# Sums of rows for seven-product blocks moved to VectorE and begun half a block ahead, norms one tile later, more lane steps per k-step

## The chip, the cores and the metric

The kernel runs on one core of one Trainium2 chip. The metric is the device time of one execution in microseconds (us). The engines are called as the profile calls them: PE is TensorE (PEld its weight load), DVE is VectorE, ACT is ScalarE, POOL is GpSimd, SP is the queue that issues most transfers. Every engine takes its instructions in the order in which they stand in its queue: an instruction that waits holds all that stand behind it.

## The reference, cut to what matters

One layer of an encoder, for two groups of tokens (256 and 1024, so 10 tiles of 128 tokens) with shared weights:

```
hn   = rms_norm(x, norm_g)
proj = hn @ w_in            # xbc, z_ssd, dt, q, k, v, z_att, mq, z_mem
y    = ssd_scan(forward) + ssd_scan(backward) + d_skip * xs
yg   = (y * silu(z_ssd)) in 2 groups of 512
o_ssd = rms_norm(yg, ssd_norm_g)
o_att = window_attention(q, k, v, sink) * silu(z_att)
o_mem = attention of mq to the normed memory * silu(z_mem)
out  = x + concat[o_ssd, o_att, o_mem] @ w_out      # 2048 x 2048
```

All of it is in float32.

## The kernel before, in words

Large products are blocks. `block_tok` makes 5 tiles of 128 tokens by up to 512 columns in 5 PSUM banks (`acc`), over 16 k-steps of 128 rows of the weight; `block_feat` does the same with features and tokens exchanged. Each float32 product is made of three products of rounded halves: ACT rounds the weight (`wh`), DVE takes the rest (`wl`), in `wsplit` (lines 215 and 216), and PE does high x high, low x high, high x low (lines 263 to 265 of `block_tok`). So a k-step of `block_tok` has 15 matmuls. The last two k-steps are done together, bank by bank, so that the evacuations are spread out. `wh` and `wl` have 3 buffers each, the raw weights 4.

The smaller work (attention, the scan, norms) runs beside the blocks. It is written as Python generators in two lanes. After each k-step, `pump` lets each lane do as many steps as `RATES` gives, a pair of numbers for each kind of block; fractions are carried on. The order in which instructions stand on each engine comes from the order in which they are written, from `high_priority` (which puts the splits and the evacuations ahead), and from the scheduler of the framework.

`ssd_up` goes up the tiles of the scan, `ssd_down` comes down them. `ssd_down(t)` loads `yd`, `zd` and the state, adds the backward part (`pyb` on PE, then `y` and `yd` on DVE), multiplies by the gate, takes the sum of squares on ACT (`yss`), makes the factor `yrs` on POOL, and scales `yd` to `yn` on DVE. `turn_ssd` transposes `yn` on PE (`pr`), copies it on ACT (`so`) and stores it in DRAM (`oT`). Tiles 9 and 8 come last of all in the lanes.

The output product `w_out` has two halves. The first 5 tiles of tokens were refilled into `xH`/`xL` (by `refill_o`, beside the block before) and run as four blocks `tok("o")`, called c=0 to c=3 here. The other 5 tiles run as 8 `block_pair`s, which make a 2 x 2 product of blocks with seven products in place of eight. These need sums of blocks on both sides: for the weights, four sums `ws` of 128x128 for each of 8 k (line 1126, on POOL), split as `sh`/`sl`; and for the rows, four sums `tt` of 128x320 for each of 8 k. One of these 8 is called a seven here. `seven_load` loads `ra` and `rb` of a seven from `oT`, `seven_sums` scales `rb` on ACT (line 1038) and makes the four sums (line 1043), `seven_rows` and `seven_split` split everything into `rH` (ACT, line 1047) and `rL` (DVE, line 1048). `ra`, `rb` and two of the five output tiles of a block (`yt`) share the 3 buffers with the tag `ch`. The rows of sevens 4 to 7 lie where the quads of `xH`/`xL` were, so that they can be written only when the last block is through with a quad.

`plan` says at which k-step of block c=3 each part is written: before, seven k has its sums and first splits at k-step 2k + 1, its loads at 2k - 1. All lanes are emptied and their memory is freed (`beside.close()`) ahead of that block.

Of the kernel before, what the change touches and what calls it, by code (L numbers as in the profile page):

```python
# [10 lines left out]
F32 = mybir.dt.float32  # L11
# [5 lines left out]
ALU = mybir.AluOpType  # L17
AX = mybir.AxisListType

P = 128  # L20
# [8 lines left out]
CH, WB, RB, WA, WBB = 3, 3, 4, 5, 4  # L29
RBB = 3  # L30

RATES = ({'q': (1.9, 0), 'kv': (1.3, 0), 'za': (1.2, 0.5), 'x': (1.1, 0.5), 'mq': (1.1, 1.2), 'zm': (1.1, 1.2),
          'z0': (1.2, 1.2), 'z1': (1.2, 1.2)},
         {'kv': (1.0, 1.0), 'x': (0.9, 1.05), 'q': (1.3, 2.3), 'za': (1.3, 2.3), 'z0': (1.5, 2.5), 'z1': (1.5, 2.5),
          'mq': (1.5, 2.6), 'zm': (1.5, 2.6), 'o': (1.7, 1.65)})
NEG = -1e30

C_X, C_Z, C_DT, C_Q, C_K, C_V, C_ZA, C_MQ, C_ZM = 0, 1536, 2560, 2592, 3104, 3232, 3360, 3872, 4384
# [4 lines left out]
def hymba_encoder_kernel(  # L43
# [24 lines left out]
    beside = ExitStack()  # L68
# [77 lines left out]
    lanes = (deque(), deque())  # L146
# [10 lines left out]
    def step(lane):  # L157
        name, gen = lane[0]
        try:

            with ExitStack() as st:
                for ins in marks:
                    st.enter_context(tc.issue_after(ins))
                next(gen)
        except StopIteration:
            lane.popleft()
            done.add(name)
# [68 lines left out]
    def w_out_rows(c):  # L236
        return w_laid(w_out_laid[c], 512)

    def block_tok(w, nt, evac, before_last=None):

        load, n = w
        ps = [acc.tile([P, 512], F32, tag="acc", name="acc") for _ in range(nt)]
        hls = {}
        for k in range(KT):
            raw = wp.tile([P, 512], F32, tag="wraw", name="wraw", bufs=RB)
            load(k, raw[:, :n])
            with tc.high_priority(offset=HP[2]):
                h = wp.tile([P, 512], F32R, tag="wh", name="wh", bufs=WB)
                l = wp.tile([P, 512], F32R, tag="wl", name="wl", bufs=WB)
                wsplit(raw[:, :n], h[:, :n], l[:, :n])  # L250
            hls[k] = h, l
            if k == KT - 2:
                continue
            if k == KT - 1 and before_last is not None:
                before_last(k)

            for t in range(nt):
                for k_ in ((k - 1, k) if k == KT - 1 else (k,)):
                    q, m = divmod(k_, 4)
                    h, l = hls[k_]  # L260
                    sh = cur["H", q][:, m, t * P:(t + 1) * P]
                    sl = cur["L", q][:, m, t * P:(t + 1) * P]
                    T.matmul(ps[t][:, :n], sh, h[:, :n], start=(k_ == 0), stop=False)  # L263
                    T.matmul(ps[t][:, :n], sh, l[:, :n], start=False, stop=False)  # L264
                    T.matmul(ps[t][:, :n], sl, h[:, :n], start=False, stop=(k_ == KT - 1))  # L265
                if k == KT - 1:
                    with tc.high_priority(offset=HP[0]):
                        evac(t, ps[t])
            if k == KT - 1:
                yield k - 1  # L270
            yield k
# [113 lines left out]
    def ev_out(c0):  # L385
        def f(t, ps):

            if t in (0, 3):
                yt = rp.tile([P, 640], F32, tag="ch", name="yt", bufs=CH)[:, :512]
            else:  # L390
                yt = ev.tile([P, 512], F32, tag="evt" if t == 2 else "evu", name="yt")
            S.dma_start(yt, xrow(t)[:, c0:c0 + 512])
            V.tensor_add(yt, ps, yt)
            S.dma_start(y_first[t * P:(t + 1) * P, c0:c0 + 512], yt)
        return f
# [550 lines left out]
        yield  # L946


    normed = deque()

    def turn_ssd():

        if normed:
            t, g, n = normed.popleft()
            ps = psum("pr")
            for j in range(4):
                T.transpose(ps[:, j * P:(j + 1) * P], n[:, j * P:(j + 1) * P], ident)
            o = mp.tile([P, 512], F32, tag="rb", name="so", bufs=RBB)
            A.activation(o, ps, AF.Copy)
            S.dma_start(oT_d[2 + g][t // 5][:, :, t % 5 * P:(t % 5 + 1) * P], hv(o, 4))  # L960

    def ssd_down(t):
        first = t in (0, NS)
        last = t in (NS - 1, NT - 1)
        tok = slice(t * P, (t + 1) * P)
        ss = sm.tile([P, 2], F32, tag="s2", name="yss", bufs=4)
        if not last:
            cc = mp.tile([P, 2, P], F32, tag="btok", name="cc", bufs=1)
            S.dma_start(cc, xbc_d[10:12, :, tok].rearrange("f p c -> p f c"))
        ld = []  # L970
        for g in range(2):
            c = slice(g * 512, (g + 1) * 512)
            y = mp.tile([P, 512], F32, tag="ya", name="yd", bufs=2)
            S.dma_start(y, yp_d[t][:, c])
            z = mp.tile([P, 512], F32, tag="xs", name="zd", bufs=2)
            S.dma_start(z, z_d[g][t])
            st = None
            if not first:
                st = state[:, c] if last else wb("st2")
                S.dma_start(st, sb_d[t][:, c])  # L980
            ld.append((y, z, st))
        turn_ssd()
        yield
        turn_ssd()
        yield
        yield
        for g in range(2):
            c = slice(g * 512, (g + 1) * 512)
            y, z, st = ld[g]
            if not last:  # L990
                pf = psum("pyb")
                T.matmul(pf, cc[:, g, :], state[:, c], start=True, stop=True)
                y2 = wb("y3")
                V.tensor_mul(hv(y2), hv(pf), hb(eacs_all[:, t, 16 + 8 * g:24 + 8 * g], 8, 64))
                V.tensor_add(y, y, y2)
            V.tensor_mul(y, y, z)
            A.activation(z, y, AF.Square, scale=rxh[:, t:t + 1], accum_out=ss[:, g:g + 1])
            if not first and not last:
                V.tensor_mul(hv(state[:, c]), hv(state[:, c]), hb(cd_all[:, t, 16 + 8 * g:24 + 8 * g], 8, 64))
                V.tensor_add(state[:, c], state[:, c], st)  # L1000
            yield
        rs = sm.tile([P, 2], F32, tag="s2", name="yrs", bufs=4)
        rsqrt(rs, ss, 1.0 / 512, 2)
        G.tensor_scalar(out=rs, in0=rs, scalar1=rxh[:, t:t + 1], scalar2=None, op0=ALU.mult)
        yield
        yield
        for g in range(2):
            n = mp.tile([P, 512], F32, tag="rf", name="yn", bufs=2)
            V.tensor_scalar(out=n, in0=ld[g][0], scalar1=rs[:, g:g + 1], scalar2=None, op0=ALU.mult)
            normed.append((t, g, n))  # L1010
        yield
        if first:
            yield
            turn_ssd()
            yield
            turn_ssd()
            yield

# [15 lines left out]
    def seven_sums(k):  # L1036
        a, b = raw[k]
        A.activation(b, b, AF.Copy, scale=vec[:, R_SG + k:R_SG + k + 1])
        a, b = hv(a, 2), hv(b, 2)
        t, u = sums[k] = [fin.tile([P, 2, 320], F32, tag="tt", name="tt", bufs=4) for _ in range(2)]  # L1040
        for o, x, y in ((t[:, 0], a[:, 1], a[:, 0]), (u[:, 0], b[:, 1], a[:, 1]), (t[:, 1], b[:, 1], t[:, 0]),
                        (u[:, 1], b[:, 0], t[:, 1])):
            G.tensor_tensor(out=o, in0=x, in1=y, op=ALU.subtract)

    def in_two(k, c, src):
        h, l = [x[:, c] for x in rows[k]]
# [14 lines left out]
        in_two(k, slice(1 + 2 * i, 3 + 2 * i), sums[k][i])  # L1061


    plan = {}
    for k in range(8):
        for j, f, args in ((-1, seven_load, ()), (1, seven_sums, ()), (1, seven_rows, ()), (2, seven_split, (0,)),
                           (3, seven_split, (1,))):

            late = k == 7 and f in (seven_rows, seven_split)
            plan.setdefault(2 * k + j + late, []).append((f, k) + args)  # L1070

    def beside_step(j):
        with ExitStack() as st:
            for ins in marks:
                st.enter_context(tc.issue_after(ins))
            for f, *args in sorted(plan.get(j, ()), key=lambda x: (x[0] is seven_load, x[1])):
                f(*args)
# [268 lines left out]
    queue(0, mem_attn, range(5, 8))  # L1346
    queue(0, mem_swap, [0])
    queue(0, mem_attn, range(8, 10))
    for c in range(3):
        tok("o", w_out_rows(c), ev_out(c * 512), grp=1)  # L1350
    for x in lanes:
        while x:
            step(x)
    beside.close()
    fin = ctx.enter_context(tc.tile_pool(name="fin", bufs=2))
    beside_step(-1)
    for k in block_tok(w_out_rows(3), 5, ev_out(1536), before_last=lambda _: beside_step(14)):
        if k != 14:
            beside_step(k)
    for u in range(8):  # L1360
        for k in block_pair(u):
            if u == 0 and k < 3:
# [70 lines left out]
```

## Time and profile before

| what | value |
|---|---|
| median of 3 runs | 1866.29 us (1865.01 to 1867.31) |
| profiled execution | 1865.38 us |
| its span, first to last instruction | 1863.7 us |
| PE busy | 1838.3 us, 99% |
| DVE / ACT / POOL busy | 1158.4 / 824.3 / 260.2 us |
| mean clock granted to PE | 0.995 |

PE is busy nearly all the time, so time is to be found where PE is idle or runs below its full clock. The rows of PE give an idle time before an instruction and who ended it. Busy shares of the other engines count only where PE waits for them. The end of a matmul is modelled, and matmuls overlap, so their pace is read from the distance of their starts.

### The profile page before, as it was taken

What the parts mean: (1) busy time and instruction counts of PE and PEld (TensorE: products, weight loads), DVE (VectorE), ACT (ScalarE), POOL (GpSimd) and SP (SyncE); (2) the same over time, 40 slices, a digit from 0 to 9 for tenths busy, and PEclk for the clock granted to TensorE, in tenths of its full rate; (3) what the DMA queues carried; (4) which work ended last, traced back from release to release, by engine and by line L of the source; (5) the groups of instructions that cost most, each with busy time, mean ns of one, the idle gap of its engine ahead of it and who ended that gap; (6) DMA issues with size and microseconds to landing.
All of it is one profiled execution on the core that took longest, in us unless ns stands there. A gap on an engine that the chain in (4) does not pass through costs nothing.

```text
span 1863.7 us, 29965 instructions
## 1 busy us (share of the span) xinstructions
PE 1838.3 (99%) x10786; PEld 1649.2 (88%) x10786; DVE 1158.4 (62%) x2284; ACT 824.3 (44%) x1865; POOL 260.2 (14%) x435
## 2 busy tenths in 40 slices
PE   9999999999999999999999999999999999989999
PEld 7889999998998889999979987777888888779999
DVE  5434555766456666586776675676875554676665
ACT  6653333434534555334345545544464442443332
POOL 0010000000000000000000000000100000577775
PEclk9999999999999999999999999999999999989999
DMA  8774444443432564434435446467685573654442
GB/s 289 236 229 128 123 148 136 136 121 95 147 125 84 171 186 142 138 101 122 129 115 169 143 128 181 122 197 216 196 253 155 169 211 115 192 161 142 142 134 88
DMA packets 198452, 289.49 MB, mean 155 GB/s; under 512 B 18912, under 2 KB 80416, under 8 KB 198304
## 3 DMA queue, kind: packets, MB, share of 16 engines
q1 hardware_dynamic: 198160, 287.53, 50.8%
q8 instruction: 85, 1.39, 0.3%
q14 instruction: 63, 0.52, 0.1%
q10 hardware_dynamic: 144, 0.06, 0.0%
HBM read 230.59 MB, written 56.92 MB: 154 GB/s over the span
## 4 chain that ended last, share of the span: by engine, by line
PE 91%; DVE 3%; DMA 2%; ACT 2%; POOL 2%; issue 1%; SPq 0%; ACTq 0%; DVEq 0%; POOLq 0%
PE acc L263 13%; PE acc L265 13%; PE acc L264 13%; PE acc L298 10%; PE acc L300 10%; PE acc L299 10%; PE acc L1143 2%; PE acc L1144 2%; PE acc L1145 2%; PE py L901 2%; PE po L648 1%; PE ppt L638 1%; PE accm L1145 1%; PE accm L1144 1%; PE pmo L749 1%
## 5 line engine op out<-in xcount | busy, mean ns | idle before, releaser
L216 DVE TENSOR_TENSOR wl<-wraw,wh 128x512 fp32r<-128x512 f32 (+2 forms) x480 | 329.6, 687 | 369.1 <-ACT wh L215 358.0
L215 ACT ACTIVATE wh<-wraw 128x512 fp32r<-128x512 f32 (+2 forms) x480 | 287.2, 600 | 503.9 <-PE acc L265 220.8
L263 PE MATMUL acc<-wh,xH 128*128 128x512 f32 (+1 forms) x1248 | 487.0, 391 | 5.7 <-ACT wh L215 4.8
L264 PE MATMUL acc<-wl,xH 128*128 128x512 f32 (+1 forms) x1248 | 474.9, 381 | 5.6 <-DVE wl L216 5.5
L265 PE MATMUL acc<-wh,xL 128*128 128x512 f32 (+1 forms) x1248 | 475.1, 381 | 0.0
L298 PE MATMUL acc<-xH,wh 128*128 128x320 f32 x1280 | 401.4, 314 | 0.0
L299 PE MATMUL acc<-xL,wh 128*128 128x320 f32 x1280 | 395.9, 309 | 0.0
L300 PE MATMUL acc<-xH,wl 128*128 128x320 f32 x1280 | 395.8, 309 | 0.0
L263 PEld LDWEIGHTS acc<-wh,xH 128*128 128x128 f32 x1248 | 235.6, 189 | 54.4 <-ACT wh L215 7.1
L264 PEld LDWEIGHTS acc<-wl,xH 128*128 128x128 f32 x1248 | 235.7, 189 | 51.5 <-DVE wl L216 9.0
L265 PEld LDWEIGHTS acc<-wh,xL 128*128 128x128 f32 x1248 | 235.4, 189 | 43.6 <-issue 0.5
L298 PEld LDWEIGHTS acc<-xH,wh 128*128 128x128 f32 x1280 | 240.4, 188 | 3.6 <-issue 3.3
L299 PEld LDWEIGHTS acc<-xL,wh 128*128 128x128 f32 x1280 | 240.4, 188 | 1.6 <-issue 1.2
L300 PEld LDWEIGHTS acc<-xH,wl 128*128 128x128 f32 x1280 | 240.2, 188 | 0.3 <-issue 0.2
L215 ACT ACTIVATE sh<-ws 128x512 fp32r<-128x512 f32 x64 | 39.7, 631 | 126.7 <-POOL ws L1126 80.6
L216 DVE TENSOR_TENSOR sl<-ws,sh 128x512 fp32r<-128x512 f32 x64 | 50.7, 792 | 67.4 <-ACT sh L215 66.5
L372 DVE SCALAR_TENSOR_TENSOR c<-u,vec,c 128x638 f32<-128x638 f32 (+1 forms) x96 | 84.7, 882 | 0.7
L1126 POOL TENSOR_TENSOR ws<-wraw 128x128 f32<-128x128 f32 x128 | 72.4, 585 | 51.6 <-DVE sl L216 32.2
L210 DVE SCALAR_TENSOR_TENSOR xL<-chd,vec,xH 128x640 fp32r<-128x640 f32 (+1 forms) x56 | 46.8, 845 | 38.2 <-ACT xH L209 37.7
L884 ACT ACTIVATE rb<-rb,wj_all 128x128 f32<-128x128 f32 x160 | 52.5, 391 | 30.0 <-DMA rb<-ac 30.0
L136 POOL TENSOR_SCALAR qr<-qss 128x8 f32<-128x8 f32 x10 | 3.5, 352 | 437.5 <-DVE qss L572 437.4
L621 ACT ACTIVATE lg<-lg,nm 128x384 f32<-128x384 f32 (+1 forms) x80 | 45.0, 563 | 40.8 <-DVE nm L615 40.8
(330 smaller groups left out, 2702.5 us busy)
## 6 DMA issues: line engine op xcount, KB each, us to landing
wraw<-in_w_in_laid_dram SPq DMA_DIRECT2D x288, 256.0 KB, 2.8
wraw<-in_w_out_laid_dram SPq DMA_DIRECT2D x64, 256.0 KB, 3.2
wraw<-in_w_out_pairs_dram SPq DMA_DIRECT2D x64, 256.0 KB, 2.8
chd<-in_x_turned_dram SPq DMA_DIRECT2D x32, 320.0 KB, 4.7
rf<-ac SPq DMA_DIRECT2D x40, 256.0 KB, 3.7
rb<-ac SPq DMA_DIRECT2D x40, 256.0 KB, 4.1
wraw<-in_w_mem_laid_dram SPq DMA_DIRECT2D x32, 256.0 KB, 4.3
xst<-in_x_sample_dram SPq DMA_DIRECT2D x32, 256.0 KB, 4.4
```

Source lines behind the costliest of these rows:

```text
L215: a = A.activation(h, raw, AF.Copy)
L216: b = V.tensor_sub(l, raw, h.bitcast(F32))
L263: T.matmul(ps[t][:, :n], sh, h[:, :n], start=(k_ == 0), stop=False)
L264: T.matmul(ps[t][:, :n], sh, l[:, :n], start=False, stop=False)
L265: T.matmul(ps[t][:, :n], sl, h[:, :n], start=False, stop=(k_ == KT - 1))
L298: T.matmul(o, sh, cur["H", q][:, m, c], start=(k == 0), stop=False)
L299: T.matmul(o, sh, cur["L", q][:, m, c], start=False, stop=False)
L300: T.matmul(o, sl, cur["H", q][:, m, c], start=False, stop=(k == KT - 1))
L372: V.scalar_tensor_tensor(out=c[:, :n], in0=u[:, k:k + n], scalar=cw[k], in1=c[:, :n], op0=ALU.mult, op1=ALU.add)
L1126: G.tensor_tensor(out=o, in0=x, in1=y, op=op)
L1144: T.matmul(ps[p], h, xl, start=False, stop=False)
L1145: T.matmul(ps[p], l, xh, start=False, stop=(k_ == 7))
```

## The change

Four things are changed together. The four sums of a seven go from POOL to DVE. The sevens begin in the middle of block c=2: sevens 0 to 3 have their sums at k-steps 2k - 5 of block c=3 (a negative number is in c=2), sevens 4 to 6 at 4k - 11, seven 7 at 15; the lanes are emptied ahead of k=8 of c=2. The norm of a tile in `ssd_down` (`norm_ssd`) is written at the start of the next tile in place of the end of its own, and its transposes two and three steps after that. And all rates from the convolution blocks on are some 4% higher.

```diff
-RATES = ({'q': (1.9, 0), 'kv': (1.3, 0), 'za': (1.2, 0.5), 'x': (1.1, 0.5), 'mq': (1.1, 1.2), 'zm': (1.1, 1.2),
+RATES = ({'q': (1.9, 0), 'kv': (1.3, 0), 'za': (1.2, 0.5), 'x': (1.15, 0.5), 'mq': (1.15, 1.25), 'zm': (1.15, 1.25),
...
-          'mq': (1.5, 2.6), 'zm': (1.5, 2.6), 'o': (1.7, 1.65)})
+          'z1': (1.55, 2.6), 'mq': (1.55, 2.7), 'zm': (1.55, 2.7), 'o': (1.75, 1.8)})
...
+    def norm_ssd():
+        if "y" in tail:
+            t, ys, rs = tail.pop("y")
+            for g in range(2):
+                n = mp.tile([P, 512], F32, tag="rf", name="yn", bufs=2)
+                V.tensor_scalar(out=n, in0=ys[g], scalar1=rs[:, g:g + 1], scalar2=None, op0=ALU.mult)
+                tail[g] = t, n
...
     def ssd_down(t):
...
+        norm_ssd()
+        yield
...
-        turn_ssd()
-        yield
-        turn_ssd()
-        yield
+        yield
+        turn_ssd(0)
+        yield
+        turn_ssd(1)
         yield
...
-        for g in range(2):
-            n = mp.tile([P, 512], F32, tag="rf", name="yn", bufs=2)
-            V.tensor_scalar(out=n, in0=ld[g][0], scalar1=rs[:, g:g + 1], scalar2=None, op0=ALU.mult)
-            normed.append((t, g, n))
+        tail["y"] = t, [x[0] for x in ld], rs
...
-            G.tensor_tensor(out=o, in0=x, in1=y, op=ALU.subtract)
+            V.tensor_sub(o, x, y)
...
-        for j, f, args in ((-1, seven_load, ()), (1, seven_sums, ()), (1, seven_rows, ()), (2, seven_split, (0,)),
-                           (3, seven_split, (1,))):
+        at = 2 * k - 5 if k < 4 else 4 * k - 11 if k < 7 else 15
+        end = at + (k == 7)
+        for j, f, args in ((at - (2 if k < 4 else 4), seven_load, ()), (at, seven_sums, ()), (end, seven_rows, ()),
+                           (end + 1, seven_split, (0,)), (end + 2, seven_split, (1,))):
...
-    for c in range(3):
+    for c in range(2):
         tok("o", w_out_rows(c), ev_out(c * 512), grp=1)
...
+    for c in range(2, 4):
+        j0 = 16 * (c - 3)
+        for k in block_tok(w_out_rows(c), 5, ev_out(c * 512), before_last=lambda _: beside_step(j0 + 14)):
+            if j0 + k == -8:
+                for x in lanes:
+                    while x:
+                        step(x)
+                beside.close()
+                fin = ctx.enter_context(tc.tile_pool(name="fin", bufs=2))
+            if j0 + k < -8:
+                pump(RATES[1]["o"])
+            elif k != 14:
+                beside_step(j0 + k)
```

The order of POOL at the end of block c=3 and the start of the pairs, before:

```order
L1043 TENSOR_TENSOR tt<-rb__17104,tt 128x320
L1126 TENSOR_TENSOR ws<-wraw 128x128 x2
L1126 TENSOR_TENSOR ws<-ws,wraw 128x128
L1126 TENSOR_TENSOR ws<-wraw,ws 128x128
L1043 TENSOR_TENSOR tt<-rb__17167,ra 128x320
L1043 TENSOR_TENSOR tt<-rb__17167,tt 128x320
L1043 TENSOR_TENSOR tt<-ra 128x320
L1043 TENSOR_TENSOR tt<-rb__17167,tt 128x320
L1126 TENSOR_TENSOR ws<-wraw 128x128 x2
```

And now, from the last `yrs` of the scan on:

```order
L1015 TENSOR_SCALAR yrs<-yrs,rxh 128x2
L1135 TENSOR_TENSOR ws<-wraw 128x128 x2
L1135 TENSOR_TENSOR ws<-ws,wraw 128x128
L1135 TENSOR_TENSOR ws<-wraw,ws 128x128
L1135 TENSOR_TENSOR ws<-wraw 128x128 x2
```

Between the sums of the weights of two k-steps stood the four sums of a seven (17167 is seven 6); now nothing stands there.

The order of DVE behind the last tile of `ssd_down` (tile 8), before, where block c=2 ends (`yt` are its evacuations) and c=3 begins:

```order
L996 TENSOR_TENSOR yd<-yd,zd 128x512
L1009 TENSOR_SCALAR yn<-yd,yrs 128x512 x2
L216 TENSOR_TENSOR wl<-wraw,wh 128x512 x2
L393 TENSOR_TENSOR yt<-acc,yt 128x512 x4
L216 TENSOR_TENSOR wl<-wraw,wh 128x512
L393 TENSOR_TENSOR yt<-acc,yt 128x512
L216 TENSOR_TENSOR wl<-wraw,wh 128x512 x2
L1048 TENSOR_TENSOR rL<-ra,rH 128x320
L216 TENSOR_TENSOR wl<-wraw,wh 128x512
L1048 TENSOR_TENSOR rL<-rb__16788,rH 128x640
```

And now, in the middle of c=2 (the `wl` are those of k=11 and 12, of 13 and of 14; 16642 is seven 0, the second `tt<-ra` belongs to seven 1):

```order
L957 TENSOR_SCALAR yn<-yd,yrs 128x512 x2
L216 TENSOR_TENSOR wl<-wraw,wh 128x512 x2
L1051 TENSOR_TENSOR tt<-ra 128x320
L1056 TENSOR_TENSOR rL<-ra,rH 128x320
L216 TENSOR_TENSOR wl<-wraw,wh 128x512
L1051 TENSOR_TENSOR tt<-rb__16642,ra 128x320
L1051 TENSOR_TENSOR tt<-rb__16642,tt 128x320
L1051 TENSOR_TENSOR tt<-ra 128x320
L1051 TENSOR_TENSOR tt<-rb__16642,tt 128x320
L1056 TENSOR_TENSOR rL<-rb__16642,rH 128x640
L1056 TENSOR_TENSOR rL<-tt,rH 128x640
L216 TENSOR_TENSOR wl<-wraw,wh 128x512
```

The sums and splits of the sevens have moved ahead of the end of c=2, and the splits of the weights for its last k-steps now stand behind sums that need `rb`. The evacuations of c=2 come further down, in the same way between sums and splits of sevens 2 and 3.

On PE, the last `pyb` of tile 8 and its transposes `pr` had 60 matmuls of c=2 between them; now there are 19, since the last steps of the lane are written at once.

More of the change, by code (lines that the diff above doesn't have):

```diff
@@ L30 @@
 RBB = 3
-RATES = ({'q': (1.9, 0), 'kv': (1.3, 0), 'za': (1.2, 0.5), 'x': (1.1, 0.5), 'mq': (1.1, 1.2), 'zm': (1.1, 1.2),
-          'z0': (1.2, 1.2), 'z1': (1.2, 1.2)},
-         {'kv': (1.0, 1.0), 'x': (0.9, 1.05), 'q': (1.3, 2.3), 'za': (1.3, 2.3), 'z0': (1.5, 2.5), 'z1': (1.5, 2.5),
-          'mq': (1.5, 2.6), 'zm': (1.5, 2.6), 'o': (1.7, 1.65)})
+RATES = ({'q': (1.9, 0), 'kv': (1.3, 0), 'za': (1.2, 0.5), 'x': (1.15, 0.5), 'mq': (1.15, 1.25), 'zm': (1.15, 1.25),
+          'z0': (1.25, 1.25), 'z1': (1.25, 1.25)},
+         {'kv': (1.05, 1.05), 'x': (0.95, 1.1), 'q': (1.35, 2.4), 'za': (1.35, 2.4), 'z0': (1.55, 2.5),
+          'z1': (1.55, 2.6), 'mq': (1.55, 2.7), 'zm': (1.55, 2.7), 'o': (1.75, 1.8)})
 NEG = -1e30
@@ L946, in ssd_up, with turn_ssd @@
         yield
[L949 to L954, printed above, removed]
+    tail = {}
+    def norm_ssd():
[5 more added lines that the diff above has]
+                tail[g] = t, n
+    def turn_ssd(g):
+        if g in tail:
+            t, n = tail.pop(g)
             ps = psum("pr")
@@ L1004, in ssd_down @@
         G.tensor_scalar(out=rs, in0=rs, scalar1=rxh[:, t:t + 1], scalar2=None, op0=ALU.mult)
+        tail["y"] = t, [x[0] for x in ld], rs
         yield
         yield
-        for g in range(2):
-            n = mp.tile([P, 512], F32, tag="rf", name="yn", bufs=2)
-            V.tensor_scalar(out=n, in0=ld[g][0], scalar1=rs[:, g:g + 1], scalar2=None, op0=ALU.mult)
-            normed.append((t, g, n))
-        yield
         if first:
+            norm_ssd()
             yield
-            turn_ssd()
             yield
-            turn_ssd()
-            yield
+            for g in range(2):
+                turn_ssd(g)
+                yield
     seven = {1: (0, 0, 0), 2: (0, 1, 5), 6: (1, 1, 2), 5: (1, 0, 1), 3: (1, 3, 6), 7: (1, 2, 3), 4: (0, 2, 4)}
@@ L1065, in hymba_encoder_kernel @@
     for k in range(8):
-        for j, f, args in ((-1, seven_load, ()), (1, seven_sums, ()), (1, seven_rows, ()), (2, seven_split, (0,)),
-                           (3, seven_split, (1,))):
-            late = k == 7 and f in (seven_rows, seven_split)
-            plan.setdefault(2 * k + j + late, []).append((f, k) + args)
+        at = 2 * k - 5 if k < 4 else 4 * k - 11 if k < 7 else 15
+        end = at + (k == 7)
+        for j, f, args in ((at - (2 if k < 4 else 4), seven_load, ()), (at, seven_sums, ()), (end, seven_rows, ()),
+                           (end + 1, seven_split, (0,)), (end + 2, seven_split, (1,))):
+            plan.setdefault(j, []).append((f, k) + args)
     def beside_step(j):
@@ L1348, in hymba_encoder_kernel @@
     queue(0, mem_attn, range(8, 10))
-    for c in range(3):
+    for c in range(2):
         tok("o", w_out_rows(c), ev_out(c * 512), grp=1)
[L1351 to L1359, printed above, removed]
+    for c in range(2, 4):
[11 more added lines that the diff above has]
+                beside_step(j0 + k)
     for u in range(8):
```

## The prediction

> **What bounds the kernel now.** I read the page's first two parts, then what TensorE waits for, then stretches, then single rows.
>
> ```profile
> PE 1838.3 (99%) x10786; PEld 1649.2 (88%) x10786; DVE 1158.4 (62%) x2284; ACT 824.3 (44%) x1865; POOL 260.2 (14%) x435
> ...
> POOL 0010000000000000000000000000100000577775
> PEclk9999999999999999999999999999999999989999
> ```
>
> TensorE (PE) is busy 99%, so only its idle time and its slow clock can be won: some 25 us of idle, and one slice of forty below full clock. That slice is where POOL first works hard, the last block of `tok("o")`, c=3. In windows of 10 us (columns: length, then busy of PE, PEld, DVE, ACT and POOL with counts, clock, DMA share, GB/s):
>
> ```profile
> 1590.00:1600.00 10.00, 10.00 (x49) 8.35 (x47) 3.92 (x6) 2.94 (x6) 0.87 (x1) 1.00 0.90 282
> ...
> 1620.00:1630.00 10.00, 8.05 (x33) 5.67 (x31) 9.00 (x9) 6.75 (x12) 7.47 (x7) 1.00 0.64 182
> ...
> 1640.00:1650.00 10.00, 6.88 (x26) 4.63 (x24) 5.19 (x6) 2.94 (x5) 7.45 (x10) 0.89 0.42 122
> 1650.00:1660.00 10.00, 7.34 (x20) 5.52 (x21) 6.96 (x9) 4.17 (x7) 8.21 (x14) 0.60 0.44 126
> ```
>
> PE does 33, 26 and 20 products where an undisturbed window has 44. The exact loss, from PE's rows in order of time (start, us, line, what, and in brackets the idle time and who ended it):
>
> ```profile
> 1576.58 0.39 PE L263 MATMUL acc<-wh,xH 128*128 128x512 f32 x1
> ...
> 1589.28 0.39 PE L265 MATMUL acc<-wh,xL 128*128 128x512 f32 x1
> ...
> 1590.30 0.48 PE L263 MATMUL acc<-wh,xH 128*128 128x512 f32 x1
> ...
> 1644.77 0.39 PE L265 MATMUL acc<-wh,xL 128*128 128x512 f32 x1
> 1645.90 0.50 PE L263 MATMUL acc<-wh,xH 128*128 128x512 f32 x1 [0.74 <-ACT wh L215]
> 1648.09 0.80 PE L264 MATMUL acc<-wl,xH 128*128 128x512 f32 x1 [1.69 <-DVE wl L216]
> ...
> 1652.34 0.80 PE L263 MATMUL acc<-wh,xH 128*128 128x512 f32 x1 [3.03 <-ACT wh L215]
> ...
> 1661.40 0.39 PE L265 MATMUL acc<-wh,xL 128*128 128x512 f32 x1
> ```
>
> The first two rows are 56 steps apart: 0.227 us for each product, 3.40 us for a k-step of 15. Block c=3 has 240 products, 54.4 us, and takes 1590.3 to 1661.6, 71.3 us: **17 us lost**. k-steps 0 to 13 (210 products, 47.6 us) end at 1645.0: 7.1 lost. The last 30 (6.8 us) take 16.6: 9.8 lost. The cause of each:
>
> ```profile
> 1619.07 0.74 ACT L1047 ACTIVATE rH<-tt 128x640 fp32r<-128x640 f32 x1 [1.96 <-POOL tt L1043]
> ...
> 1620.79 0.61 ACT L215 ACTIVATE wh<-wraw 128x512 fp32r<-128x512 f32 x1
> ```
>
> ```profile
> 1644.26 0.88 POOL L1043 TENSOR_TENSOR tt<-rb__17167,ra 128x320 f32<-128x320 f32 x1
> ...
> 1647.45 1.31 POOL L1043 TENSOR_TENSOR tt<-rb__17167,tt 128x320 f32<-128x320 f32 x1
> ...
> 1650.65 0.45 POOL L1126 TENSOR_TENSOR ws<-wraw,ws 128x128 f32<-128x128 f32 x1
> ```
>
> ```profile
> 1651.14 0.63 ACT L215 ACTIVATE sh<-ws 128x512 fp32r<-128x512 f32 x1 [4.66 <-POOL ws L1126]
> 1651.67 0.61 ACT L215 ACTIVATE wh<-wraw 128x512 fp32r<-128x512 f32 x1
> ```
>
> Early in the block the weight split `wh` stands on ScalarE (ACT) behind `rH<-tt`, which waits for POOL's sums. At the end it stands behind `sh`, which waits for `ws`, and POOL does four sums of seven 6 first (1644.26 to 1648.76).
>
> **The sums on VectorE, half a block ahead.** The 32 sums leave POOL, so the late 9.8 us lose their cause: behind `ws` on POOL there is only `ws`. Cover if I am wrong: none, `sh` stays ahead of `wh` on ACT. Prices on DVE:
>
> ```profile
> 1628.66 1.50 DVE L1048 TENSOR_TENSOR rL<-rb__17041,rH 128x640 fp32r<-128x640 f32 x1
> ...
> 1632.77 0.68 DVE L216 TENSOR_TENSOR wl<-wraw,wh 128x512 fp32r<-128x512 f32 x1
> ...
> 1664.06 0.69 DVE L393 TENSOR_TENSOR yt<-acc,yt 128x512 f32<-128x512 f32 x1 [0.43 <-DVE wl L216]
> 1664.66 0.48 DVE L1048 TENSOR_TENSOR rL<-ra,rH 128x320 fp32r<-128x320 f32 x1
> 1665.06 0.82 DVE L1048 TENSOR_TENSOR rL<-rb__17230,rH 128x640 fp32r<-128x640 f32 x1
> ```
>
> A sum has the shape of the 0.48 row; a 640-wide split takes 1.50 while POOL sums and 0.82 while POOL rests. I take 0.82, since POOL now rests until the pairs' `ws`: a seven costs 4 x 0.48 + 0.48 + 3 x 0.82 = 4.9 us of DVE. The Trainium skill (SBUF — State Buffer, Who interferes with whom) says that a DVE instruction with two SBUF inputs and a POOL instruction that reads SBUF lock each other out; the two rows agree. If 1.50 were the split's own price, the two and a half sevens before the block's edge would cost 2.5 x 3 x 0.68 = 5 us more, and the sum would gain 11 in place of 16.
>
> The new cost is in c=2. The lanes must end before its k=8, so the last six steps of `ssd_down(8)` are issued at once, and the first sevens follow their stores:
>
> ```profile
> 1575.03 1.02 PE L992 MATMUL pyb<-state,cc 128*128 128x512 f32 x2
> ...
> 1589.51 1.04 PE L957 MATMUL pr<-ident,yn 128*128 128x128 f32 x8
> ```
>
> ```profile
> 1581.02 0.89 DVE L1009 TENSOR_SCALAR yn<-yd,yrs 128x512 f32<-128x512 f32 x2 [2.34 <-POOL yrs L1004]
> ```
>
> ```profile
> 1591.48 4.22 DMA oT<-so
> 1595.72 4.27 DMA rb__16788<-oT
> 1600.01 0.84 ACT rb__16788 L1038
> 1600.92 4.81 POOL tt L1043 x4
> ```
>
> Count from the last `pyb`. Its first `yn` is there after 6.4 us (1581.02 + 0.44 - 1575.03). In the new order 19 products stand between it and `pr` (60 before): PE arrives at 0.8 + 19 x 0.227 = 5.1 and waits **1.4**. From `pr` to the scaling of rb is 10.5 us (1589.51 to 1600.01), so at 16.9. After it on DVE stand four sums, two splits, then `wl` of k=14, done at 17.7 + 1.9 + 1.6 + 0.7 = 22.0; PE wants it at 0.8 + six steps of 3.4 + 1.0 + 1.4 = 23.6: hidden. rb of seven 1 has the buffer of ra of seven 0 (three for all), free at 18.2; it lands 2.9 later by its median:
>
> ```profile
> rb__16852<-oT SPq DMA_DIRECT2D x1, 320.0 KB, 2.9
> ```
>
> With issue and scaling that is 22.3. Then a split, two sums, a split, a sum, a split and `wl` of k=15 make 26.2; PE wants it at 24.5: **1.7**. Over the block's edge DVE does 1.5 more sevens, two `wl` and five `yt`; its fifth `yt` ends at 36.7, and PE wants that bank at 34.9: **1.9**. Ends: 0, if the transfers are quick, to 9, if rb takes the 4.27 of the row above and each wait grows by that 1.4. Later sevens have four steps each (13.6 us against 4.9 + 2.7): hidden. Moved to SP's queue, rb of seven 0 waits for the store 4.2 us with two weight loads of c=3 behind it, wanted 15 us later: hidden. So 17.0 - 5.0 = **12.0 won**.
>
> A wait may slow the clock besides. The row at 1648.09 is already 0.80 long after 0.74 and 1.69 of idle, and the clock came back at about 1658, some 2 us lost. The Trainium skill (TensorE: Matmul & The Clock Gate, Part 1: The HAM clock gate) halves the clock after an idle window of about 3.4 us; here two waits with 2.4 us in them did it. By its figure my waits of 1.4, 1.7 and 1.9 cost no clock.
>
> **Norms a tile later.**
>
> ```profile
> PE pr L957 <- DVE yn L1009: 3.3, 4, 1.3
> PE psc L606 <- ACT cb L796: 2.1, 1, 2.1
> ```
>
> ```profile
> 1288.41 0.63 PE L957 MATMUL pr<-ident,yn 128*128 128x128 f32 x4 [1.28 <-DVE yn L1009]
> ```
>
> The same VectorE and POOL work moves one lane step back, so it costs nothing by itself; next tile's `yd` loads wait for `yn` as before, one step behind it. In the new order PE has 9 to 15 us of products, by their count, between `pyb` and `pr`, where the four that wait have 6.5 to 11; one tile has only 6.8, as little as that of the 1288.41 row, so it pays 1.3 again. **2.0 won** (0 to 3.3).
>
> **Rates.** Some 4% more lane steps for a k-step change no amount of work. Most of the program has PE at 100% and stays. The one place is the refill for `o`, where PE's other large loss is:
>
> ```profile
> 1374.00:1380.00 6.00, 3.11 (x11) 2.10 (x11) 5.19 (x14) 5.46 (x12) 0.00 (x0) 0.85 0.75 248
> 1380.00:1386.00 6.00, 6.00 (x23) 4.89 (x22) 4.15 (x13) 3.33 (x11) 0.00 (x0) 0.58 0.79 239
> ```
>
> 2.9 idle and 6 us at 0.58 of the clock, 5.4 lost: `cb` stood on ACT behind splits that waited for loads. In the new order `cb` comes after one such split, not after six. But the loads are as many and DMA is no faster, so I take half, **2.5** (-3 to 5.4).
>
> Sum: 12.0 + 2.0 + 2.5 = 16.5. The profiled execution took 1865.4 us (span 1863.7): 1848.9. The median of the runs is 0.9 above it, so **1850**.
>
> **Rivals.** (1) *The load sets the pace, not POOL.* DVE's queue is then blocked by rb as it was by POOL, the 7.1 us only move, and 9.8 are won: 9.8 + 2.0 - 1.4 - 1.9 = 8.5, 1858. For it: three buffers for two tiles a seven. Against it: a seven needs 0.84 + 1.9 + 2.9 = 5.6 us, under its 6.8. (2) *All goes well*: the waits of 1.7 and 1.9 are absorbed, the refill's loss goes whole: 17.0 - 1.4 + 3.3 + 5.4 = 24.3, 1842. Against it: DVE is full over the block's edge. (3) *Slower: SP's queue.* Each rb waits for its buffer with weight loads behind it; if each of the eight holds PE for one load, 8 x 2.9 = 23 us are lost in place of 17 + 2 + 2.5 won: with 1.4 + 1.9 more, 1871. It decides from 2.3 us for each seven. Against it: weights are loaded four k-steps ahead, 13.6 us. (4) *It doesn't do what it says*: half of the sevens are held so, the gain is eaten: 1866.
>
> **How the numbers follow.** Forecast 0.50, rival 1 0.22, rival 2 0.13, rival 3 0.07, rival 4 0.08. 0.2% (3.7 us) is what can be told from no change. Forecast and rivals 1 and 2 are faster by more: 0.85; same 0.08, slower 0.07. The range goes from rival 2 to rival 1 with 2 us of slack, 1842 to 1860; the likeliest one's own is 1845 to 1854.
>
> **What would show it.** c=3 in about 56 us with no wait for `sh` or `wh` at its end; splits of 0.82; one wait of 1 to 2 us at `pr` in c=2, one at its k=15, some on `yt`; `pr` waits of 1 to 2 us in all before; the clock near 1380 above 0.9. I am wrong if c=2's second half loses over 9 us, if POOL's `ws` still holds ACT at c=3's end, or if a new dip of the clock stands anywhere before 1500.

## The result, and the profile after

| | before | after |
|---|---|---|
| median | 1866.13 us (4 runs, 1865.01 to 1867.31) | 1852.91 us (4 runs, 1852.35 to 1856.93) |
| ratio, 95% interval | | 0.9934 (0.9917 to 0.9951) |
| profiled execution, its span | 1865.38, 1863.7 us | 1852.38, 1850.7 us |
| mean clock granted to PE | 0.995 | 0.999 |

The page of after; none of its 40 slices has less than nine tenths of the clock any more, and POOL works later and less:

```profile
PE 1831.2 (99%) x10786; PEld 1646.6 (89%) x10786; DVE 1161.2 (63%) x2316; ACT 827.0 (45%) x1865; POOL 224.2 (12%) x403
...
POOL 0011010000000000000000000001100000057774
PEclk9999999999999999999999999999999999999999
```

PE in order of time in after: the first products of c=3, of pair 0 (L1152, the `block_pair`), a row in it, and the first of pair 1.

```profile
1588.37 0.39 PE L263 MATMUL acc<-wh,xH 128*128 128x512 f32 x1
...
1643.27 0.39 PE L1152 MATMUL acc<-rH,wh 128*128 128x320 f32 x1 [0.34 <-ACT rH L1055]
...
1649.67 0.64 PE L1152 MATMUL acc<-rH,sh 128*128 128x320 f32 x1 [2.48 <-DVE yt L393]
...
1673.57 0.30 PE L1152 MATMUL acc<-rH,wh 128*128 128x320 f32 x1
```

And the same of before, for pair 0:

```profile
1661.63 0.31 PE L1143 MATMUL acc<-rH,wh 128*128 128x320 f32 x1
...
1687.22 0.30 PE L1143 MATMUL acc<-rH,wh 128*128 128x320 f32 x1
```

Block c=3 takes 1643.27 - 1588.37 = 54.9 us, where it took 71.3 (1590.30 to 1661.63): 16.4 won. It begins 1.9 earlier than before. Pair 0 takes 30.3, where it took 25.6: 4.7 given back. The end gives back 0.6. 1.9 + 16.4 - 4.7 - 0.6 = 13.0, the difference of the spans. So nearly all of the gain came out of one block, and over a quarter of it was lost again in the block behind.

Windows of after over c=3 and pair 0 (columns as ahead of the result): c=3 has its 45 or 46 products in every full window; then PE loses 3.5 us, and the clock dips.

```profile
1590.00:1600.00 10.00, 10.00 (x46) 8.29 (x45) 7.88 (x14) 5.09 (x8) 0.00 (x0) 1.00 0.92 280
...
1640.00:1650.00 10.00, 6.54 (x30) 4.78 (x30) 7.46 (x14) 4.20 (x8) 4.04 (x7) 0.98 0.54 164
1650.00:1660.00 10.00, 10.00 (x60) 10.00 (x60) 6.79 (x10) 3.14 (x6) 7.23 (x12) 0.85 0.69 225
```

The cause in pair 0, from SP's queue and then from DVE in after. `yt` of tile t=3 of c=3 lies in the buffers `ch` that the sevens and two output tiles share:

```profile
1643.19 1.34 SPq L394 DMA_DIRECT2D out_dram<-yt  x2
1645.65 0.34 SPq L392 DMA_DIRECT2D yt<-in_x_sample_dram  x1
```

```profile
1642.49 0.68 DVE L393 TENSOR_TENSOR yt<-acc,yt 128x512 f32<-128x512 f32 x1
...
1648.92 0.69 DVE L393 TENSOR_TENSOR yt<-acc,yt 128x512 f32<-128x512 f32 x1 [2.54 <-issue]
```

Tile t=0 is added at 1642.49 and stored from 1643.19; only then does its buffer come free, x of t=3 is loaded at 1645.65 and added at 1648.92, and the PSUM bank that pair 0 wants comes free with that. In before the chain was the same (its last add is the 1664.06 row of the prediction), but PE was so late itself that it lost 0.3 us to it.

### The profile page after: what moved, and what is told of

Same layout as the page of the kernel before. It is cut to its first block, busy times and chain, and to the rows that moved or that the text cites. A ratio compares the mean times of both kernels' runs of the same rounds, so it can differ in the third digit from the quotient of the medians.

```text
span 1850.7 us, 29984 instructions
## 1 busy us (share of the span) xinstructions
PE 1831.2 (99%) x10786; PEld 1646.6 (89%) x10786; DVE 1161.2 (63%) x2316; ACT 827.0 (45%) x1865; POOL 224.2 (12%) x403
## 4 chain that ended last, share of the span: by engine, by line
PE 91%; DMA 3%; DVE 2%; ACT 1%; issue 1%; POOL 1%; SPq 0%; ACTq 0%; DVEq 0%; POOLq 0%
PE acc L263 13%; PE acc L265 13%; PE acc L264 13%; PE acc L298 10%; PE acc L300 10%; PE acc L299 10%; PE acc L1152 3%; PE acc L1153 3%; PE acc L1154 3%; PE py L901 2%; PE po L648 1%; PE ppt L638 1%; PE accm L1154 1%; PE accm L1153 1%; PE accm L1152 1%
## 5 line engine op out<-in xcount | busy, mean ns | idle before, releaser
L216 DVE TENSOR_TENSOR wl<-wraw,wh 128x512 fp32r<-128x512 f32 (+2 forms) x480 | 323.8, 675 | 353.3 <-ACT wh L215 346.3
L216 DVE TENSOR_TENSOR sl<-ws,sh 128x512 fp32r<-128x512 f32 x64 | 51.6, 806 | 64.8 <-ACT sh L215 63.9
L1135 POOL TENSOR_TENSOR ws<-wraw 128x128 f32<-128x128 f32 x128 | 73.4, 593 | 121.0 <-ACT wh L215 62.9
L1152 PE MATMUL acc<-rH,sh 128*128 128x320 f32 x192 | 60.0, 312 | 2.8 <-DVE yt L393 2.8
```

Of the source, the lines that this page charges most:

```text
L216: b = V.tensor_sub(l, raw, h.bitcast(F32))
L1152: T.matmul(ps[p], h, xh, start=(k_ == 0), stop=False)
```

## The experiments

Eleven kernels, each against before on the same chip. c=2, c=3 and pair 0 are read as above, from the start of a block's first product to the next block's, in the profiled execution. A pair that loses nothing takes 24.66 us (as pairs 1 to 6 do in every kernel), c=3 54.4. The length of c=2 holds the lanes' products that fall into it, so that it isn't a loss by itself. "The lead" is the half block by which the sevens begin earlier. The early loss of c=3 is that of k-steps 0 to 13, the late loss that of its last 30 products.

| kernel | median us | ratio (interval) | c=2 | c=3 | pair 0 |
|---|---|---|---|---|---|
| before | 1866.1 | | 69.6 | 71.3 | 25.6 |
| after | 1852.9 | 0.9934 (0.9917 to 0.9951) | 64.4 | 54.9 | 30.3 |
| s1 after, sums on POOL | 1860.8 | 0.9970 (0.9959 to 0.9981) | 66.9 | 60.2 | 27.7 |
| s2 before, sums on DVE | 1856.2 | 0.9953 (0.9938 to 0.9968) | 69.8 | 58.4 | 30.2 |
| s3 after, old rates | 1856.8 | 0.9948 (0.9933 to 0.9963) | 70.6 | 57.9 | 30.5 |
| s4 after, old norms | 1852.3 | 0.9923 (0.9908 to 0.9937) | 62.9 | 55.0 | 30.7 |
| s5 after, own buffer for `yt` | 1847.6 | 0.9899 (0.9882 to 0.9915) | 64.8 | 55.0 | 26.3 |
| s6 after, old norms and rates | 1858.8 | 0.9962 (0.9947 to 0.9977) | 71.4 | 57.9 | 30.5 |
| s7 as s5, rate of `o` 2.0 | 1845.6 | 0.9892 (0.9875 to 0.9908) | 62.9 | 55.3 | 26.2 |
| s8 before, new norms and rates | 1856.0 | 0.9949 (0.9934 to 0.9964) | 63.2 | 63.7 | 26.1 |
| s9 after, no lead | 1852.1 | 0.9934 (0.9920 to 0.9949) | 64.4 | 55.7 | 31.6 |
| s10 before, new rate of `o` alone | 1859.1 | 0.9970 (0.9958 to 0.9982) | 65.4 | 64.1 | 25.6 |
| s11 as s9, own buffer for `yt` | 1848.0 | 0.9911 (0.9898 to 0.9924) | 63.7 | 55.4 | 26.5 |

**s1, sums back on POOL, all else as in after.**

```diff
-            V.tensor_sub(o, x, y)
+            G.tensor_tensor(out=o, in0=x, in1=y, op=ALU.subtract)
```

> The changed kernel, with the 32 sums of the sevens back on POOL; the plan that begins half a block ahead stays. Theory (engine): sevens 6 and 7 have the same k-steps as before, so POOL's sums stand ahead of the second ws again and hold ACT at the end of c=3: most of the 9.8 us come back there, and a seven takes 0.84 + 4.8 + 2.9 = 8.5 us against two k-steps of 6.8, so sevens 0 to 3 run late by some us more: 1861 to 1866 us, c=3 (54.9 us in the changed kernel) 62 to 68. Rival (lead): it is the half block of lead that counts, the engine is immaterial: 1852 to 1855, c=3 at 55 to 57.

1860.8, and c=3 60.2: just below what the engine's theory gave, far above the lead's. But the theory had the place wrong: the early loss is 4.1 us, and the late one, where most of the 9.8 us were to come back, is 1.7 (0.5 in after). Windows of s1, then the row of PE in them with the longest wait:

```profile
1590.00:1600.00 10.00, 8.41 (x35) 6.34 (x36) 7.06 (x11) 2.88 (x5) 2.01 (x2) 1.00 0.76 244
1600.00:1610.00 10.00, 7.58 (x32) 5.74 (x31) 6.20 (x8) 6.36 (x11) 7.27 (x7) 1.00 0.75 239
1610.00:1620.00 10.00, 10.00 (x46) 8.27 (x45) 5.43 (x7) 3.72 (x7) 1.93 (x2) 1.00 0.66 219
```

```profile
1604.63 0.50 PE L263 MATMUL acc<-wh,xH 128*128 128x512 f32 x1 [1.99 <-ACT wh L215]
```

While a seven has two k-steps the products fall to 35 and 32; from 1610 to the end of k-step 13, where a seven has four, none is lost. How much of the early loss is POOL's pace is not told by this, since rb of seven 3 came late too (it was scaled at 1600.10, after 5.2 us in which ACT waited for its load).

The end of c=3 in s1, the first `ws` on POOL and the `sh` that stands behind the sums of seven 6, and the first `ws` in before:

```profile
1633.57 1.41 POOL L1135 TENSOR_TENSOR ws<-wraw 128x128 f32<-128x128 f32 x2 [9.22 <-DMA wraw<-in_w_out_pairs_dram]
```

```profile
1642.86 0.63 ACT L215 ACTIVATE sh<-ws 128x512 fp32r<-128x512 f32 x1 [4.74 <-POOL ws L1135]
```

```profile
1642.47 0.88 POOL L1126 TENSOR_TENSOR ws<-wraw 128x128 f32<-128x128 f32 x2 [3.74 <-DMA wraw<-in_w_out_pairs_dram]
```

`sh` waits as long as in before (4.66), behind the same four sums, and PE loses little by it. What differs is when this work begins: the pairs' first weights are loaded while PE is at k-step 10 and summed at k-step 11 in s1, at 12 and 13 in before (and in s8 and s10, where the late loss is nearly whole). No run changes that start alone.

With the lead, VectorE is worth 7.9 us in medians (1860.8 to 1852.9), 5.3 between the profiled executions. The rest goes with the clock, which was 1.000 in s1's profiled execution and 0.996 to 0.999 in eight of its other nine.

**s2, the sums on DVE and nothing else**: the diff of s1 turned round, on the kernel before.

> The kernel before, with the 32 sums on DVE and nothing else changed (no lead, old norms, old rates). Theory (engine and lead add up): with sums on POOL and the lead, c=3 took 60.2 us, with both changed 54.9, before 71.3; the engine alone takes away the late cause (9.8 us) and makes a seven 2.9 us shorter, so c=3 comes to 58 to 62 us, and pair 0 waits some 5 us for its fourth evacuated tile as in the changed kernel: 1857 to 1861 us. Rival (lead): of the 16.4 us won in c=3 the engine is worth the 5.3 that it was worth with the lead, c=3 stays at 65 to 67: 1861 to 1864.

1856.2, faster than the theory had it. c=3 takes 58.4, as expected, with the lanes still ending at its edge. That alone removes the early loss, though the first rb comes no sooner than before; the row (minimum, median and maximum in ns, then its start) and the window behind it in s2:

```profile
L1038 ACT ACTIVATE rb__16788<-rb__16788,vec x1: 832/832/832, 1598.6 to 1598.6; 128x640 f32<-128x640 f32 x1
```

```profile
1600.00:1610.00 10.00, 10.00 (x45) 8.27 (x45) 9.73 (x18) 8.19 (x14) 0.00 (x0) 1.00 0.70 217
```

DVE is full there but makes up the delay without holding PE. The late loss is 3.9 us.

**s3, the rates of before in after** (the lines of `RATES` as they were).

> The changed kernel with the rates of before. Theory: the rates are worth little by themselves, but 13 steps of lane 1 (nearly all of ssd_down(8), its loads among them) are then forced at once ahead of k=8 of c=2, and PE waits there for loads of 2.9 to 4.3 us besides the 1.3 us chain: 4 to 8 us lost in c=2, 1856 to 1861 us. Rival: the scheduler spreads the forced steps over the splits and PE waits no more than now: 1851 to 1854.

1856.8: the rates are worth 4 us. The number is the theory's, the place isn't: from c=1's start to c=3's PE waits 1.1 us in all, 1.3 in after. By c=3's start it stands 1.3 us behind after, by longer waits ahead of c=1, and c=3 loses 3.0 more. What PE waited for in s3 (us, times, longest), two lines of the groups:

```profile
PE acc L263 <- DVE yt L393: 2.2, 2, 1.7
PE pr L966 <- DVE yn L957: 2.0, 2, 1.1
```

The steps left over at k=8 of c=2 are issued at once there, and what follows on DVE (the evacuations `yt` at the block's edge) comes late.

**s4, the norms as before in after** (`turn_ssd` and `ssd_down` of before).

> The changed kernel with norms and transposes of ssd_down where they were before. The prediction's theory (2.0 us won by the later norm): 1855, with pr waits of some 5 to 6 us in all ahead of c=2. Rival, from the trace after (pr waits 3.1 us ahead of c=2, 3.3 before): the later norm wins nothing, 1852 to 1853.5, pr waits the same within 1 us.

1852.3: nothing is lost without the new norms. The sum of the waits at `pr` in s4, and in after:

```profile
PE pr L957 <- DVE yn L1009: 4.1, 5, 1.4
```

```profile
PE pr L966 <- DVE yn L957: 4.4, 4, 1.4
```

**s5, a buffer of its own for the last `yt` of c=3.** The one with the tag `tt` is one of the sums' four.

```diff
+            if t == 3 and c0 == 1536:
+                yt = fin.tile([P, 2, 320], F32, tag="tt", name="yt", bufs=4).rearrange("p a c -> p (a c)")[:, :512]
-            if t in (0, 3):
+            elif t in (0, 3):
```

> The changed kernel, and in the last block c=3 the fourth evacuated tile (t=3) takes a buffer of the sums (tag tt) in place of one of the three ch buffers, so that its load need not wait until the first tile's store is out. Theory: pair block 0, which takes 30.3 us (25.6 before, 24.7 for the others), waits 2.5 us for that tile's chain store - load - add, and loses 2 more to the clock after it: 26 to 27 us with the buffer, 1848.5 to 1850 in all. Rival: pair 0 waits because DVE and ACT are full there (sevens 6 and 7 with the weights' splits), so the wait only moves to the next bank: 29 to 30 us, 1852 to 1853.

1847.6, pair 0 26.3 in place of 30.3. In s5 PE's longest wait in pair 0, and the window in which after has 0.85 of the clock:

```profile
1646.29 0.42 PE L1154 MATMUL acc<-rH,sh 128*128 128x320 f32 x1 [0.42 <-DVE yt L395]
```

```profile
1650.00:1660.00 10.00, 10.00 (x70) 10.00 (x69) 5.48 (x7) 3.42 (x7) 8.00 (x14) 1.00 0.64 213
```

So 4.0 of the 4.7 us were the chain store, load, add in one shared buffer, and the clock that went with the wait.

**s6, the sevens alone** (s3's and s4's edits together on after).

> The changed kernel with norms and rates of before: only the sevens (sums on DVE, half a block ahead, lanes emptied ahead of k=8 of c=2). Theory: the rates earn their 4 us by what they leave to be forced at k=8 of c=2, the norms nothing, so the same as with old rates alone: 1856 to 1858 us, with c=2 at 69 to 71 us (64.4 in the changed kernel). Rival: the old norms fit the old rates and the 4 us come from somewhere ahead of the output blocks: 1852 to 1854.

1858.8, a little above the theory, where s2, the same without the lead, has 1856.2: with the old rates the lead brings nothing. c=3 starts 2.9 us later than in before, and c=2 takes 71.4.

**s7, s5 and more lane steps in `o`** (`'o': (1.75, 2.0)`), so that no step is left at k=8 of c=2.

> The kernel with the other buffer for t=3 (1847.6 us), and lane 1 at 2.0 in place of 1.8 steps for each k-step of the output blocks, so that no step is left to be forced at k=8 of c=2. Theory: the wait of 1.3 us at the last pr goes, 1846 to 1847, pr waits 1.3 us less. Rival: the wait moves to another place of the lanes (its chain is as long wherever it stands), 1847 to 1849.

1845.6, the best of all, 20 us below before. The waits at `pr` in s7, and in s5:

```profile
PE pr L968 <- DVE yn L959: 3.3, 3, 1.6
```

```profile
PE pr L968 <- DVE yn L959: 4.6, 4, 1.6
```

The wait of 1.3 us in c=2 is gone, c=2 is 1.9 shorter, and c=3 begins 1.8 earlier than in s5.

**s8, new norms and rates, the sevens as before.**

> The kernel before with the new norms and the new rates, the sevens as before. The prediction's theory: 4.5 us won ahead of c=2, 1861 to 1862. Rival, from the traces (block c=1 begins 0.3 us earlier in the changed kernel than in the one before): nothing won, 1865 to 1867, with pr waits of 3 us and c=3 at 70 to 72 us.

Both theories missed: 1856.0, and c=3 in 63.7 with POOL making the sums as before. The early loss was gone without any of the edits that were meant for it. A new theory: the early 7.1 us of before came from the lanes. With more steps they end sooner, so the last tile of the scan is stored sooner, and the first rb is there when c=3 begins. The smallest edit that does this is one pair of numbers:

**s10, the rate of `o` alone in before.**

```diff
-           'mq': (1.5, 2.6), 'zm': (1.5, 2.6), 'o': (1.7, 1.65)})
+           'mq': (1.5, 2.6), 'zm': (1.5, 2.6), 'o': (1.75, 1.8)})
```

> The kernel before with one pair of numbers changed: the rates beside tok("o") from 1.7, 1.65 to 1.75, 1.8. Sums stay on POOL, sevens stay in c=3, norms stay. With it 45 products stand between the last pyb and the last pr, and 300 of 315 stand between that pr and the pairs that stood at the edge before: the lanes end five k-steps (17 us) ahead of c=3. Theory: the early loss of c=3 (7.1 us in k-steps 0 to 13) was never POOL's pace but the late end of the lanes, which let the first rb land 10 us into c=3. Then c=3 takes 63 to 65 us in place of 71.3 with POOL still making the sums, its first rb is scaled within 3 us of its start, and the time is 1855 to 1859. Rival: norms and the earlier rates brought what norms and rates brought together; then c=3 still takes 70 us or more and the time is 1863 to 1866.

c=3 in 64.1, as the new theory had it; the time, 1859.1, at its upper end. From PE in s10, the last `pr`, the start of c=3, its longest wait and its end; then the first scaling of rb on ACT, and two windows:

```profile
1573.72 0.27 PE L957 MATMUL pr<-ident,yn 128*128 128x128 f32 x1
...
1591.61 0.39 PE L263 MATMUL acc<-wh,xH 128*128 128x512 f32 x1
...
1646.53 0.80 PE L263 MATMUL acc<-wh,xH 128*128 128x512 f32 x1 [3.53 <-ACT wh L215]
...
1655.73 0.31 PE L1143 MATMUL acc<-rH,wh 128*128 128x320 f32 x1
```

```profile
1593.38 0.84 ACT L1038 ACTIVATE rb__16788<-rb__16788,vec 128x640 f32<-128x640 f32 x1 [0.74 <-DVE yt L393]
```

```profile
1600.00:1610.00 10.00, 10.00 (x46) 8.29 (x45) 7.58 (x8) 6.61 (x11) 7.24 (x7) 1.00 0.64 206
...
1640.00:1650.00 10.00, 4.29 (x9) 2.59 (x10) 7.63 (x9) 4.83 (x9) 8.28 (x12) 0.76 0.42 111
```

The last `pr` comes 18 us ahead of c=3 (before: at its edge), rb is scaled 1.8 us into c=3 (before: 9.7), and with POOL at 7.24 of 10 PE loses nothing. The late loss stays whole: 9 products in the window at 1640. So the two losses of c=3 had different causes. Why the time is 3 us above s8's is the earlier part of the program: c=3 begins at 1591.6, in s8 at 1586.8, and 3.4 of these 4.8 us are the clock, which fell to half at the refill in s10's profiled execution and not in s8's.

**s9, after without the lead** (the plan and the last loops of before).

> The changed kernel with the plan and the last loops of before: sums on VectorE, new norms, new rates, but the sevens begin in c=3. Theory: with the lanes ending five k-steps ahead of c=3 and the sums off POOL, the lead of half a block is worth next to nothing: c=2 about 63 us (no forced steps), c=3 about 58 (the end still waits for seven 7's and the weights' work on ACT, as with sums on VectorE alone), pair 0 about 30, in all 1850 to 1854 against 1852.9. Rival: the lead is what carries the gain; then 1856 or more, as with VectorE's sums alone (1856.2).

1852.1 against 1852.9: the lead is worth nothing that can be told. c=3 loses 1.3 us, not the 4 that s2 had and that the theory expected again. s9 and s8 differ in nothing but the engine of the sums, and the late loss is 1.3 and 8.6 us: without the lead it is the engine that takes it away.

**s11, s9 with the buffer of s5.**

> The kernel without the lead, and the last output tile of c=3 (t=3) gets a buffer of its own (tag tt) in place of ch. Theory: pair 0 falls from about 30 to 26 us and the time by 3 to 4 us against the kernel without the lead, so about 1847 to 1850. Rival: without the lead the buffer tt is still taken by the sums of sevens 6 and 7 when t=3 wants it, so that x comes as late as from ch: no change.

1848.0, pair 0 26.5: the shared buffer costs 4 to 5 us with and without the lead.

All the sevens' kernels side by side, in medians:

| sums, norms and rates | sevens in c=3 | half a block ahead |
|---|---|---|
| POOL, old | 1866.1 (before) | not run |
| POOL, new | 1856.0 (s8) | 1860.8 (s1) |
| DVE, old | 1856.2 (s2) | 1858.8 (s6) |
| DVE, new | 1852.1 (s9) | 1852.9 (after) |

In no row does the lead gain. The sums alone, or norms and rates alone, bring 10 us each, together 14 (each against the before that ran beside it: 9.5, 9.7 and 13.4).

## Why the prediction was right, point by point

**The loss of c=3** (17.0, all of it won): 16.4 measured. The size held, the causes in part. In the late half `ws` stands alone on POOL now, and ACT's `sh` and `wh` no longer hold PE; the engine does that by itself (8.6 us in s8, 1.3 in s9). But s1 keeps POOL's four sums ahead of `ws` and loses only 1.7, with the pairs' weights two k-steps sooner, so that order was not enough to lose the 9.8 us. How much of them came from the late start of this work stays open. The early half's cause was only its last link. The chain that I read (`wh` behind `rH<-tt` behind POOL's sums) is in the trace, but s10 removes it with POOL's sums in place. POOL's pace was enough; it could not make up a start 10 us late, and DVE (s2) could. What I worked out against rival 1, the time of one seven's load, didn't touch this: not the loads' pace but their first start was late.

**The split of 0.82 beside a POOL at rest**: right. The groups of `rL` in after (minimum, median and maximum in ns):

```profile
L1056 DVE TENSOR_TENSOR rL<-tt,rH x16: 809/820/1084, 1575.6 to 1652.8; 128x640 fp32r<-128x640 f32 x16
...
L1056 DVE TENSOR_TENSOR rL<-ra,rH x8: 483/486/747, 1570.5 to 1649.5; 128x320 fp32r<-128x320 f32 x8
```

The 1.50 was POOL's doing (in s1, with the sums back on POOL, it is there again), so the 5 us that hung on it were not due.

**The waits in c=2** (1.4, which by its own 6.4 - 5.1 is 1.3, then 1.7 and 1.9): the first was right, the other two are zero. PE, then DVE, SP, ACT and DVE once more, all of after:

```profile
1557.89 1.02 PE L1003 MATMUL pyb<-state,cc 128*128 128x512 f32 x2
...
1564.52 1.06 PE L966 MATMUL pr<-ident,yn 128*128 128x128 f32 x8 [1.28 <-DVE yn L957]
```

```profile
1563.89 0.88 DVE L957 TENSOR_SCALAR yn<-yd,yrs 128x512 f32<-128x512 f32 x2 [2.35 <-POOL yrs L1015]
```

```profile
1565.80 1.47 SPq L969 DMA_DIRECT2D oT<-so  x2
1569.19 0.33 SPq L1042 DMA_DIRECT2D rb__16642<-oT  x1
```

```profile
1572.38 0.83 ACT L1046 ACTIVATE rb__16642<-rb__16642,vec 128x640 f32<-128x640 f32 x1 [0.19 <-DMA rb__16642<-oT]
```

```profile
1580.33 0.69 DVE L216 TENSOR_TENSOR wl<-wraw,wh 128x512 fp32r<-128x512 f32 x1
```

`yn` came 6.4 us behind `pyb` (1563.89 + 0.44 - 1557.89), PE waited 1.28 for it, and no other wait follows up to pair 0. From `pr` to the scaling of rb I took 10.5 us from the edge of before, where DMA was at 0.90; here, at 0.37 to 0.67 between 1560 and 1580, it was 7.9 (3.4 from the store's issue to the load's, some 3 to land). So `wl` of k=15 ended 23.1 us behind `pyb`, not 26.2, and PE wanted it at 24.5. The term that was mis-sized is that of the transfers: a landing time from a crowded stretch was carried to an emptier one (that it is shorter is measured; that the emptier queues made it so is not tested). No wait for `yt` came at the edge of c=2. One came a block later, by another chain, and cost pair 0 its 4.7 us: no step of the prediction asked what the pairs wait for once c=3 ends on time.

**Norms and refill** (2.0 and 2.5): by c=3's start after is 1.9 us ahead of before, with the wait of 1.3 paid, so 3.2 were won, not 4.5. The norms' share is nothing (s4): their waits add to 4.4 us where they added to 3.3. What was won is the clock of the refill. It is whole in after, in the two windows where before had 0.85 and 0.58:

```profile
1374.00:1380.00 6.00, 4.13 (x27) 3.32 (x25) 4.12 (x9) 3.78 (x8) 0.00 (x0) 1.00 0.79 243
1380.00:1386.00 6.00, 5.95 (x31) 4.37 (x32) 5.74 (x18) 4.66 (x15) 0.00 (x0) 1.00 0.63 202
```

PE's idle times from its first products to c=1 add to 9.1 us, before to 9.5: the wait of 2.1 for `cb` is gone, and one of 1.9 for `pT` has come. Nor is the clock surely the change's doing. s2's program is that of before in all but the engine of the sums, which come 200 us later. In s2 PE waits as long for `cb`, and the clock stays whole:

```profile
1379.55 0.39 PE L606 MATMUL psc<-kT,qT 128*128 128x256 f32 x1 [2.11 <-ACT cb L796]
```

```profile
1380.00:1386.00 6.00, 6.00 (x33) 4.70 (x32) 5.92 (x17) 4.84 (x16) 0.00 (x0) 1.00 0.90 229
```

With the rates of before the clock fell there in three profiled executions (before, s6, s10) and not in two (s2, s3); with the new rates it fell in none of eight. So the new rates may help, but how much of the 3.2 us is luck isn't told.

"Changes no amount of work" was the step that failed for the rates: they also say where the lanes end. The pair beside `o`, which decides this, went up by 3% and 9%, not by some 4%. By s10 that is worth some 6 us where POOL makes the sums, by s3 all rates are worth 4 us beside all the rest.

The sum then was 16.4 + 3.2 - 1.3 - 4.7 - 0.6 = 13.0 against 16.5, and the time 2.9 us above the forecast: two costs that weren't there (3.6 us), and one of like size that was not seen (4.7). That these two nearly cancel is luck. Rivals 3 and 4 fell: no weight load was late, and c=3 lost 0.5 us.

## What to carry to other kernels

The wait that a trace names last may be only the end of a chain: ask whether the engine it names is too slow or merely began late, and test the start (here one pair of numbers) apart from the engine. When a slow block is mended, follow the next one at its new time; a chain of store, load and add through a shared buffer was harmless only while PE was late. Where several parts of a change work on the same stretch, run each alone and with one left out, since here two of them brought 10 us each and 14 together, and a third nothing. And before a change is credited with a dip of the clock that is gone, ask whether every run of the old code has it.

## What the runs showed of the hardware that was not expected

The clock can fall after waits as short as those that the prediction took to cost none, and it doesn't come back at once. PE in s9, the waits at the start of pair 0, and four windows of 2 us behind them:

```profile
1642.92 0.39 PE L1152 MATMUL acc<-rH,wh 128*128 128x320 f32 x1 [1.17 <-ACT wh L215]
...
1645.54 0.63 PE L1152 MATMUL acc<-rH,sh 128*128 128x320 f32 x1 [0.36 <-DVE yt L393]
...
1649.33 0.63 PE L1152 MATMUL acc<-rH,sh 128*128 128x320 f32 x1 [1.55 <-DVE yt L393]
```

```profile
1643.00:1645.00 2.00, 1.73 (x9) 1.23 (x9) 2.00 (x5) 1.34 (x3) 0.61 (x1) 1.00 0.76 289
1645.00:1647.00 2.00, 1.64 (x7) 1.46 (x6) 1.04 (x2) 0.00 (x0) 1.81 (x4) 0.57 0.59 131
...
1653.00:1655.00 2.00, 2.00 (x9) 2.00 (x9) 0.56 (x1) 0.00 (x0) 1.92 (x4) 0.50 0.96 360
1655.00:1657.00 2.00, 2.00 (x14) 2.00 (x13) 0.68 (x1) 1.05 (x2) 1.55 (x4) 0.87 0.23 86
```

With idle times of 1.17 and 0.36 us (and one of 0.28 between them) the clock is at half from about 1645.3 to 1655.4, though PE is fed without a break from 1649.33 on. In s1 a wait of 1.99 cost no clock (1.00 in the window at 1600). The same code can go either way: at the refill PE waits 0.79 and 2.10 us in before, 0.65 and 2.11 in s2, and the clock is at half for some 7 us in before and whole in s2. The Trainium skill (TensorE: Matmul & The Clock Gate, Part 1: The HAM clock gate) puts the fall behind an idle window of about 3.4 us; by that, s9 would have kept its clock, so here the rows decide against it. What makes one run of short waits tip the clock and another not, these runs don't tell. The spread goes with it: s1, with waits of this kind, ran from 1857.1 us (clock 1.000) to 1865.1 (0.996), s7, with fewer, from 1845.0 to 1846.3 (1.000 each time).
